# A hybrid decoder layer on one core: gated unit and gates projected for all tokens ahead of the mixers

## The chip, the cores and the metric

The kernel runs on one core of a Trainium2 chip. A core has TensorE (PE, matrix products into PSUM), VectorE (DVE), ScalarE (ACT), GpSimd (POOL) and SyncE (SP, which issues DMAs here), each with its own in-order list of instructions; they wait for each other on semaphores. The metric is the device time of one execution in microseconds, lower is better.

## What is computed

One layer on 1024 tokens of width 1024, in float32. The input is normalised (h), projected by one matrix, mixed by two branches, gated, projected and normalised again; then a feed-forward block with a 3-tap causal convolution.

```python
u = h @ w_in   # columns: conformer GLU (a, g) | z | x, B, C | dt | gate_a | gate_b
# conformer branch
v = a * sigmoid(g)
v = causal_dwconv(v, 31 taps)            # per channel, over positions
y_a = silu(layer_norm(v)) @ w_conv_out
# state-space branch: 4-tap causal conv and silu on x, B, C; dt = softplus(dt + bias)
# scan in chunks of 128 tokens, 4 groups of 8 heads, a state carried from chunk to chunk
y = scan(x, dt, B, C) + x * d_skip
y = y * silu(z); y = y * rsqrt(mean(y^2 per group))
y_b = (y * norm_w) @ w_ssm_out
# join
h = LN(alpha*h + (sigmoid(gate_a)*y_a + sigmoid(gate_b)*y_b) @ w_o)
h = LN(alpha*h + ConvFFN(h))
```

## The kernel before

**Precision.** Every float32 operand of a large product is split into a rounded part and a rest (ScalarE casts, VectorE subtracts), and a product is three matmuls (`mm3`, L180 to L182): part by part, part by rest, rest by part. A projection of one tile of 128 columns on 512 tokens (`project`) has 8 blocks along the width, so 24 matmuls. `weights` (L141) loads a tile of weights by SP into `wst` (three buffers) and splits it into `wsp` (three buffers).

**Two halves.** The tokens are worked off in two halves of 512, up to the first norm. `ln_first` (half 0) or `ln_in` (half 1) normalises four row tiles and transposes them into hT. `mixers` then projects dt, then for each of four groups g: B, C and four x tiles, each with the 4-tap convolution `conv4`; at g = 3 the first half of the state-space output, `ssm_out_first` (weights `w_so`, eight projections); two GLU tiles (`glu`, four projections, `w_ga` and `w_gg`); the scan `ssd_group`; in it at the end z (`z_gate`, four projections); and at low priority the 31 taps of the two GLU tiles (`conv31`, L545, 30 operations of 512 tokens each, the tail of half 0 kept in `v_halo`). After the loop come the eight tiles of gate a, their sigmoids sent to DRAM, with the last group's normalisation (`done(yT)`) behind the second of them.

`combine` projects the eight tiles of gate b and, interleaved, the second half of the state-space output (`w_sp`, which needs yT). It loads the tap results (tiles `cc`), normalises them over the channels (sums over tiles by POOL, L768 to L781; sums over partitions by TensorE), splits them into sT, and projects them (`w_co`); the joined result mixT goes to `out_proj`.

**The scan** of a group has four chunks in a row. A chunk transposes x (L593), loads a tile m of cumulated decays by POOL (L602, two buffers), turns it into decays on ScalarE (L607, L611) and VectorE (L623), updates the state (L632, L639) and multiplies (L642). At the end of a group come the skip, the gate, the squares, a sum by TensorE (L672), and a factor that goes out to DRAM and back (L680, L681).

**The feed-forward block** (`ffn_blocks`, `up_first`, `up_pair`, `down`) multiplies already by blocks: two column tiles of weights and all 1024 tokens make a 2 x 2 block product with seven products of half the width (12 matmuls each) in the place of eight. It needs sums of weight blocks (VectorE, L991 to L994) and of token blocks (made once, kept in `h1b` and `h1s`). For the first LEAD = 8 pairs the two products that need only the first half of the tokens are computed early (`up_first`), sent to DRAM and loaded again.

**Order.** The instructions of each engine are put in order ahead of time by a planner, by priority (the place in the program, moved by `tc.high_priority(offset=...)`) and by simulated readiness. Within `tc.manual_schedule` the named engines keep the program's order. Pools opened on the same side of the memory lie one on another, and a tile waits for the earlier tiles whose memory it takes. PSUM has two rings of four banks: `acc` for projections, `sm` for the scan and transposes.

Of the kernel before, what the change touches and what calls it, by code (L numbers as in the profile page):

```python
# [16 lines left out]
P = 128  # L17
D = 1024
# [6 lines left out]
LEAD = 8  # L25
HEADS = 32
# [28 lines left out]
def kernel(  # L55
# [39 lines left out]
    mean_stack = ExitStack()  # L95
    mean_w = mean_stack.enter_context(pool("mean", side="right")).tile([P, P], F32, name="mean_w")
    V.memset(mean_w, 1.0 / D)
    state_stack = ExitStack()
    statep = state_stack.enter_context(pool("states", side="right"))
    upper = statep.tile([P, P], F32, name="upper")  # L100
    make_upper_triangular(nc, upper, 1.0, diag=True)
    later = statep.tile([P, P], F32, name="later")
    make_lower_triangular(nc, later, 1.0, diag=False)
    ones = statep.tile([P, P], F32, name="ones")
    V.memset(ones, 1.0)
# [3 lines left out]
    a_log = statep.tile([P, HEADS], F32, name="a_log")  # L109
    nskip = statep.tile([P, 2, 16], F32, name="nskip")  # L110
    pick = statep.tile([P, 4, 4], F32, name="pick")
    V.memset(pick, 0.0)
    for c in range(4):
        V.memset(pick[:, c, c : c + 1], 1.0)
    u_halo = statep.tile([P, 24, 3], F32, name="u_halo")
    G.memset(u_halo, 0.0)
    v_halo = statep.tile([P, 8, KC - 1], F32, name="v_halo")
    G.memset(v_halo, 0.0)
    fold = statep.tile([2 * HEADS, HEADS], F32, name="fold")
    V.tensor_add(fold, ident[: 2 * HEADS, :HEADS], ident[: 2 * HEADS, HEADS : 2 * HEADS])  # L120
    states = [statep.tile([P, HALF], F32, name=f"state{g}") for g in range(GROUPS)]
    dts = [statep.tile([P, 4, HEADS], F32, name=n) for n in ("dtv", "wds")]
    edc = statep.tile([P, 2, 4, HEADS], F32, name="edc")
    cums = statep.tile([P, 4, HEADS], F32, name="cums")
# [10 lines left out]
    g_scr = [dram.tile([8, P, HALF], F32, name=f"g_scr{i}") for i in range(2)]  # L135
# [115 lines left out]
    def ln_first():  # L251

        hT = big_tile("hT0")
        et = mybir.EngineType
        with pool("lnin0", side="right") as pl:
            xts, raw = [], []
            with tc.high_priority(offset=8000), tc.manual_schedule(
                engines={et.Activation, et.DVE, et.PE}
            ):
                A.activation(out=pl.tile([P, 1], F32, name="warm"), in_=eps, func=AF.Sqrt)  # L260
                for t in range(4):
                    xt = pl.tile([P, D], F32, tag="x", bufs=4, name=f"x0_{t}")
                    SY.dma_start(xt, x[t * P : (t + 1) * P, :])
                    xts.append(xt)
                    if t == 1:
                        gb = [row(pl, RW_ING, D, "in_g"), row(pl, RW_INB, D, "in_b")]
                    for ct in ((), (), (CT_DT, CT_B), (CT_C,))[t]:
                        raw.append(raw_weights(ct, f"first{ct}"))
                SY.dma_start(pc[:, :PC_N], pcol[:, :PC_N])
                SY.dma_start(a_log, prow[RW_AL : RW_AL + HEADS].partition_broadcast(P))  # L270
                SY.dma_start(nskip.rearrange("p i k -> p (i k)"), pcol[:, PC_N:])
                mvs = [pl.tile([P, 1, 2], F32, name=f"mv_in{t}") for t in range(4)]
                rss = [pl.tile([P, 1], F32, name=f"rs_in{t}") for t in range(4)]
                work = pl.tile([P, D], F32, name="ln_work")
                pts = {}

                def stats(t):
                    st = pl.tile([P, 2, 6], F32, name=f"st_in{t}")
                    for q in range(2):
                        ln_part(pl, xts[t], st, q)  # L280
                    V.bn_aggr(out=mvs[t][:, 0, :], in_=st)
                    A.activation(out=rss[t], in_=mvs[t][:, :, 1], func=AF.Sqrt, bias=eps)

                def sums(t):
                    mean, var = mvs[t][:, 0, 0:1], mvs[t][:, 0, 1:2]
                    A.activation(out=work, in_=xts[t], func=AF.Identity, accum_out=var)
                    A.mul(mean, var, -1.0 / D)
                    A.activation(out=work, in_=xts[t], func=AF.Square, bias=mean, accum_out=var)
                    A.activation(out=rss[t], in_=var, func=AF.Sqrt, bias=eps, scale=1.0 / D)

                def norm(*ts):
                    for t in ts:
                        V.reciprocal(out=rss[t], in_=rss[t])
                        V.scalar_tensor_tensor(
                            out=xts[t], in0=xts[t], scalar=mvs[t][:, 0, 0:1], in1=gb[0],
                            op0=ALU.subtract if t < 2 else ALU.add, op1=ALU.mult,
                        )
                    for t in ts:
                        V.scalar_tensor_tensor(
                            out=xts[t], in0=xts[t], scalar=rss[t], in1=gb[1],  # L300
                            op0=ALU.mult, op1=ALU.add,
                        )
                        store(t)

                def store(t):
                    SY.dma_start(h_scr[0][t * P : (t + 1) * P, :], xts[t])

                def hi(t):
                    pts[t] = [transposed(xts[t], q) for q in (0, 4)]
                    for q, pt in zip((0, 4), pts[t]):  # L310
                        A.copy(hT[:, 0, q : q + 4, t * P : (t + 1) * P], pt)

                def lo(t):
                    for q, pt in zip((0, 4), pts[t]):
                        ks, ts = slice(q, q + 4), slice(t * P, (t + 1) * P)
                        V.tensor_tensor(
                            out=hT[:, 1, ks, ts], in0=pt, in1=hT[:, 0, ks, ts].bitcast(F32),
                            op=ALU.subtract,
                        )

                pss = [bank(1) for _ in range(3)]
                ws = []

                def columns(i, q, parts):
                    ts = slice(q * 256, (q + 1) * 256)
                    n = len(parts)
                    for m, (a, b) in enumerate(parts):
                        for k in range(KD):
                            if i:
                                w, ps = ws[i][:, a, k * P : (k + 1) * P], pss[i][:, ts]  # L330
                            else:
                                w, ps = ws[0][:, k, :], pss[0][: 2 * HEADS, ts]
                            TE.matmul(  # L333
                                ps,
                                w,
                                hT[:, b, k, ts],
                                start=(a, b) == (0, 0) and k == 0,
                                stop=(a, b) == (1 if i else 0, 0 if i else 1) and k == KD - 1,
                            )

                stats(0)
                stats(1)
                norm(0, 1)
                sums(2)
                hi(0)
                lo(0)
                ws.append(weights_side_by_side(raw[0], "c0_dt"))
                hi(1)
                lo(1)
                columns(0, 0, ((0, 0), (0, 1)))  # L350
                ws.append(split_weights(raw[1], "c0_b"))
                columns(1, 0, ((0, 0), (0, 1), (1, 0)))
                norm(2)
                sums(3)
                ws.append(split_weights(raw[2], "c0_c"))
                norm(3)
                hi(2)
                columns(2, 0, ((0, 0), (0, 1), (1, 0)))
                lo(2)
                hi(3)  # L360
                lo(3)
                for i in range(3):
                    columns(i, 1, ((0, 0), (0, 1)) + (((1, 0),) if i else ()))
        return hT, pss

    def ln_in():
        hT = big_tile("hT1")
        with pool("lnin1", side="right") as pl:
            xts = []
            with tc.high_priority(offset=6000):  # L370
                for t in range(4):
                    xt = pl.tile([P, D], F32, tag="x", bufs=4, name=f"x1_{t}")
                    SY.dma_start(xt, x[HALF + t * P : HALF + (t + 1) * P, :])
                    xts.append(xt)
# [138 lines left out]
    def glu(pl, hh, hT, i):  # L513
# [10 lines left out]
        if hh == 0:  # L524
            A.copy(v_halo[:, i, :], v[:, HALF:])
# [891 lines left out]
```

## Time and profile before

| | us |
|---|---|
| median of 3 runs | 1954.16 (1954.07 to 1954.42) |
| span of the profiled execution | 1951.6 |
| PE busy | 1926.3 (99%), 9128 matmuls |
| DVE busy | 1633.5 (84%) |
| ACT busy | 1105.9 (57%) |
| POOL busy | 133.7 (7%) |

The profile is of one execution. The runs' median is 2.6 us above its span, which goes from the first to the last instruction. Matmuls are pipelined: one of 512 columns is shown with about 0.39 us, but they follow each other more closely, so spacing, not duration, tells what one costs. The same holds, less so, for VectorE. A row of a timeline gives start, duration, engine, line, operation, result and operands; in brackets the idle time before it and what ended it. A row of grouped instructions gives count, total busy time and the mean duration of one in ns.

### The profile page before, as it was taken

What the parts mean: (1) busy time and instruction counts of PE and PEld (TensorE: products, weight loads), DVE (VectorE), ACT (ScalarE), POOL (GpSimd) and SP (SyncE); (2) the same over time, 40 slices, a digit from 0 to 9 for tenths busy, and PEclk for the clock granted to TensorE, in tenths of its full rate; (3) what the DMA queues carried; (4) which work ended last, traced back from release to release, by engine and by line L of the source; (5) the groups of instructions that cost most, each with busy time, mean ns of one, the idle gap of its engine ahead of it and who ended that gap; (6) DMA issues with size and microseconds to landing.
All of it is one profiled execution on the core that took longest, in us unless ns stands there. A gap on an engine that the chain in (4) does not pass through costs nothing.

```text
span 1951.6 us, 24929 instructions
## 1 busy us (share of the span) xinstructions
PE 1926.3 (99%) x9128; PEld 1575.7 (81%) x9128; DVE 1633.5 (84%) x2215; ACT 1105.9 (57%) x1841; POOL 133.7 (7%) x184
## 2 busy tenths in 40 slices
PE   7999999999999999999999999999999999999998
PEld 6888888887888887888888888888888888888886
DVE  7799999997666889999999956588998887878778
ACT  6767777664453367877765545365655454453442
POOL 0100000000400010000000040001000000011000
PEclk9999999999999999999999999999999999999999
DMA  6434343534546542424353454576443332368572
GB/s 223 132 114 130 108 136 118 177 100 141 178 128 215 207 131 96 143 104 136 107 174 108 139 180 129 159 267 243 156 157 108 113 103 90 113 230 268 180 253 108
DMA packets 104011, 297.68 MB, mean 153 GB/s; under 512 B 12432, under 2 KB 12464, under 8 KB 103888
## 3 DMA queue, kind: packets, MB, share of 16 engines
q1 hardware_dynamic: 87840, 244.68, 37.5%
q0 software_dynamic: 13744, 47.21, 7.8%
q10 hardware_dynamic: 2304, 4.20, 0.6%
q8 instruction: 71, 1.16, 0.3%
q14 instruction: 52, 0.43, 0.1%
HBM read 246.22 MB, written 49.82 MB: 152 GB/s over the span
## 4 chain that ended last, share of the span: by engine, by line
PE 78%; issue 11%; DVE 5%; DMA 3%; ACT 2%; POOL 1%; SPq 0%; DVEq 0%; ACTq 0%; POOLq 0%
PE acc L181 21%; PE acc L180 21%; PE acc L182 21%; PE sm L180 3%; PE sm L182 3%; PE sm L181 3%; PE sm L642 2%; PE sm L628 1%; PE sm L632 1%; DMA do<-wdown 1%; PE sm L593 1%; PE acc L333 1%; DMA m<-cum_scr 1%; DVE w_dn L1193 1%; DVE rows L244 1%
## 5 line engine op out<-in xcount | busy, mean ns | idle before, releaser
L545 DVE SCALAR_TENSOR_TENSOR c<-v,pc,c 128x512 f32<-128x512 f32 x480 | 346.1, 749 | 6.8 <-ACT c L534 5.6
L180 PE MATMUL acc<-hT,w_c 128*128 128x512 f32 x368 | 147.2, 400 | 0.0
L181 PE MATMUL acc<-hT,w_c 128*128 128x512 f32 x368 | 146.9, 399 | 0.0
L182 PE MATMUL acc<-hT,w_c 128*128 128x512 f32 x368 | 144.9, 394 | 0.0
L607 ACT ACTIVATE m<-m,cums 128x128 f32<-128x128 f32 x256 | 79.0, 398 | 64.5 <-DMA m<-cum_scr 60.7
L1052 DVE SCALAR_TENSOR_TENSOR fo<-u,pc,fo 128x1024 f32<-128x1024 f32 x88 | 111.3, 1289 | 0.0
L500 DVE SCALAR_TENSOR_TENSOR xbc<-u,pc,xbc 128x512 f32<-128x512 f32 x144 | 105.9, 751 | 1.1 <-ACT xbc L498 0.9
L180 PE MATMUL acc<-h1s,w_s 128*128 128x512 f32 x264 | 103.4, 392 | 0.2 <-ACT u L1036 0.2
L182 PE MATMUL acc<-h1s,w_s 128*128 128x512 f32 x264 | 103.0, 390 | 0.0
L182 PE MATMUL acc<-hT,w_z 128*128 128x512 f32 x256 | 102.8, 402 | 0.0
L181 PE MATMUL acc<-h1s,w_s 128*128 128x512 f32 x264 | 102.7, 389 | 0.0
L180 PE MATMUL acc<-hT,w_z 128*128 128x512 f32 x256 | 101.9, 398 | 0.4 <-ACT sig L521 0.4
L1192 ACT CAST w_dn<-dr 128x1024 fp32r<-128x1024 f32 (+1 forms) x73 | 60.7, 843 | 72.1 <-DVE dr L1122 42.5
L181 PE MATMUL acc<-hT,w_z 128*128 128x512 f32 x256 | 101.1, 395 | 0.0
L181 PEld LDWEIGHTS acc<-hT,w_c 128*128 128x128 f32 x368 | 69.2, 188 | 16.3 <-issue 3.1
L1193 DVE TENSOR_TENSOR w_dn<-dr,w_dn 128x1024 fp32r<-128x1024 f32 (+1 forms) x73 | 70.2, 971 | 13.8 <-ACT w_dn L1192 13.6
L182 PEld LDWEIGHTS acc<-hT,w_c 128*128 128x128 f32 x368 | 69.2, 188 | 15.6 <-issue 1.9
L180 PEld LDWEIGHTS acc<-hT,w_c 128*128 128x128 f32 x368 | 69.2, 188 | 15.5 <-issue 1.9
L147 DVE TENSOR_TENSOR w_c<-st_c,w_c 128x1024 fp32r<-128x1024 f32 x46 | 56.1, 1219 | 19.3 <-ACT w_c L146 19.3
L146 ACT CAST w_c<-st_c 128x1024 fp32r<-128x1024 f32 x46 | 48.3, 1051 | 40.7 <-PE acc L182 18.4
L180 PE MATMUL sm<-h1b,w_s 128*128 128x512 f32 x176 | 69.1, 393 | 0.0
L181 PE MATMUL sm<-h1b,w_s 128*128 128x512 f32 x176 | 69.0, 392 | 0.0
(382 smaller groups left out, 5596.2 us busy)
## 6 DMA issues: line engine op xcount, KB each, us to landing
st_c<-wcol SPq DMA_DIRECT2D x46, 512.0 KB, 3.5
st_z<-wz SPq DMA_DIRECT2D x32, 512.0 KB, 3.5
m<-cum_scr POOLq DMA_DIRECT2D x32, 512.0 KB, 4.7
st_wo<-wo SPq DMA_DIRECT2D x24, 512.0 KB, 4.1
ra<-wup SPq DMA_DIRECT2D x22, 512.0 KB, 3.8
rb<-wup SPq DMA_DIRECT2D x22, 512.0 KB, 3.3
t_scr<-fo POOLq DMA_DIRECT2D x22, 512.0 KB, 3.4
dr<-t_scr SPq DMA_DIRECT2D x44, 256.0 KB, 4.0
```

Source lines behind the costliest of these rows:

```text
L146: A.copy(w[:, 0, :], st)
L147: (eng or V).tensor_tensor(out=w[:, 1, :], in0=st, in1=w[:, 0, :].bitcast(F32), op=ALU.subtract)
L180: TE.matmul(ps, wa(0), xa(0), start=start, stop=False, skip_group_check=more)
L181: TE.matmul(ps, wa(0), xa(1), start=False, stop=False, skip_group_check=more)
L182: TE.matmul(ps, wa(1), xa(0), start=False, stop=stop, skip_group_check=more)
L500: V.scalar_tensor_tensor(out=o, in0=u[:, k : k + HALF], scalar=pc[:, wc + k : wc + k + 1], in1=o, op0=ALU.mult, op1=ALU.add,)
L545: V.scalar_tensor_tensor(out=accs[i], in0=v[:, k : k + HALF], scalar=pc[:, wc + k : wc + k + 1], in1=accs[i], op0=ALU.mult, op1=ALU.add,)
L607: A.activation(out=m[:, h, :], in_=m[:, h, :], func=AF.Relu, scale=-1.0, bias=cums[:, c, k : k + 1],)
L642: TE.matmul(py[h % 2 * HP : (h % 2 + 1) * HP, h // 2 * P : (h // 2 + 1) * P], xs[:, h * HP : (h + 1) * HP], m[:, h, :], start=True, stop=True,
L1052: V.scalar_tensor_tensor(out=o, in0=u[:, k : k + T], scalar=pc[:, wc + k : wc + k + 1], in1=o, op0=ALU.mult, op1=ALU.add,)
L1192: A.copy(w[:, 0, cs], src)
L1193: V.tensor_tensor(out=w[:, 1, cs], in0=src, in1=w[:, 0, cs].bitcast(F32), op=ALU.subtract)
```

## The change

**GLU and gates ahead of the mixers.** The 16 GLU tiles and the 16 gate tiles leave `mixers` and `combine`. They become 16 pairs of column tiles (eight pairs (a_i, g_i), four of gate a, four of gate b), each computed for all 1024 tokens by the seven block products that the feed-forward block has used, before the first mixer. The helpers are made general for it: `block_maker` (block sums of the tokens), `pair_first`, `pair_weights`, `pair`, `all_pairs`.

- `head` replaces `ln_first`: it normalises and transposes the first four row tiles, then, between the two early products of the first LEAD1 = 12 pairs, normalises the other four and makes the block sums. The columns dt, B, C of half 0 are no longer computed there; `first_columns` does so in both mixers.
- After each pair, `glu_and_gates` takes the sigmoid and, for GLU, the product with 1024 tokens, and sends the result to DRAM (`v_scr`, `g_scr`) by POOL.
- `ln_in` of half 1 loads the normalised rows from DRAM and only transposes and splits.

**Taps.** `conv31` now takes one channel tile, loads v from DRAM and stores by POOL. For four of the eight tiles (WHOLE = 4) it runs over all 1024 tokens (30 operations each), issued after the pairs 1, 5, 9 and 13 at lowered priority, with one buffer each for v and c. The other four run in halves in the mixers, one per group.

**Mixers and combine.** `done(yT)` of the last group stands directly behind the loop; the gates are loaded from DRAM. The constants and states of the scan are allocated after the pairs.

```diff
-                vs = [(i, glu(pl, hh, hT, i)) for i in (2 * g, 2 * g + 1)]
                 done = ssd_group(pl, hh, g, xT, BT, CT, lambda: z_gate(pl, hh, hT, g))
-                with tc.high_priority(offset=-1500):
-                    conv31(pl, hh, vs)
+                if WHOLE + g < 8:
+                    with tc.high_priority(offset=-1500):
+                        conv31(pl, WHOLE + g, hh * HALF, HALF)
+            done(yT)
+        return yT
...
             for j in range(8):
-                pg = bank(1)
-                project(pg, weights(wcol[CT_GA + j], f"gt{hh}_{j}"), hT)
-                ga = pl.tile([P, HALF], F32, tag="ya", bufs=2, name=f"gt{hh}_{j}")
-                A.activation(out=ga, in_=pg, func=AF.Sigmoid)
-                SY.dma_start(g_scr[hh][j], ga)
-                if j == 1:
-                    done(yT)
...
                 gb = pl.tile([P, HALF], F32, tag="gate", bufs=3, name=f"gb{hh}_{j}")
-                A.activation(out=gb, in_=pg, func=AF.Sigmoid)
+                SY.dma_start(gb, g_scr["gb"][j][:, hs])
...
+    def glu_and_gates(j, ug, uv):
+
+        if j < 8:
+            A.activation(out=uv, in_=uv, func=AF.Sigmoid)
+            V.tensor_mul(ug, ug, uv)
+            G.dma_start(v_scr[j], ug)
+            return
+        scr = g_scr["ga" if j < 12 else "gb"]
+        for i, u in enumerate((ug, uv)):
+            A.activation(out=u, in_=u, func=AF.Sigmoid)
+            G.dma_start(scr[2 * (j % 4) + i], u)
...
+        for t in range(4):
+            with tc.high_priority(offset=4000):
+                load(4 + t)
+            for j in range(3 * t, 3 * t + 3):
+                if j == 3 * t + (1 if t else 2):
+                    mv, rs = ln_stats(tp, [xts[4 + t]], f"in1_{t}")
+                    ln_apply(xts[4 + t], mv, rs, 0, *gb)
+                    store(4 + t)
+                    second_rows(t, xts[4 + t], V)
+                if j not in ws:
+                    lead_weights(j)
+                pair_first(fp, bl, first1_scr, j, [ws[j][:, i] for i in range(2)])
...
+    with pool("pairs1") as p1:
+        us = [p1.tile([P, T], F32, name=f"u1_{i}") for i in range(4)]
+        with pool("whole", side="right") as cp:
+
+            def taps(j):
+                if j % 4 == 1:
+                    with tc.high_priority(offset=-600):
+                        conv31(cp, j // 4, 0, T)
+
+            all_pairs(p1, us, 0, bl, first1_scr, srcs1, LEAD1, "p", None, glu_and_gates, taps)
+    st1.close()
...
-    yT = mixers(0, hT, pre)
+    yT = mixers(0, hT)
```

More of the change, by code (lines that the diff above doesn't have):

```diff
@@ L108 @@
     pc = const.tile([P, PC_N + 88], F32, name="pc")
[L109 to L124, printed above, removed]
     h_scr = [dram.tile([HALF, D], F32, name=f"h_scr{i}") for i in range(2)]
@@ L249, in ln_apply @@
         )
-    def ln_first():
-        hT = big_tile("hT0")
-        et = mybir.EngineType
[L255 to L364, printed above, removed]
@@ L1042, in up_pair, with all_pairs, made, taps_and_product @@
         V.tensor_tensor(out=uv[:, early], in0=pz, in1=s, op=ALU.subtract)
+        then(j, ug, uv)
+    def all_pairs(pl, us, off, bl, scr, srcs, lead, name, ws, then, after=None):
+        n = len(srcs)
+        def made(j, ws=None):
+            ws = ws or pair_weights(pl, srcs, j, lead, name)
+            return pair(pl, us, off, bl, scr, j, ws, then)
+        with tc.manual_schedule(engines={mybir.EngineType.PE}):
+            pairs = [made(0, ws)]
+            next(pairs[0])
+            next(pairs[0])
+            for j in range(1, n + 1):
+                if j < n:
+                    pairs.append(made(j))
+                    next(pairs[j])
+                next(pairs[j - 1], None)
+                if j < n:
+                    next(pairs[j])
+                if after:
+                    after(j - 1)
+    def glu_and_gates(j, ug, uv):
[8 more added lines that the diff above has]
+            G.dma_start(scr[2 * (j % 4) + i], u)
+    def taps_and_product(upp, kept, j, ug, uv):
         os = []
@@ L1276 @@
+    states = [statep.tile([P, HALF], F32, name=f"state{g}") for g in range(GROUPS)]
+    dts = [statep.tile([P, 4, HEADS], F32, name=n) for n in ("dtv", "wds")]
+    edc = statep.tile([P, 2, 4, HEADS], F32, name="edc")
+    cums = statep.tile([P, 4, HEADS], F32, name="cums")
+    SY.dma_start(a_log, prow[RW_AL : RW_AL + HEADS].partition_broadcast(P))
+    SY.dma_start(nskip.rearrange("p i k -> p (i k)"), pcol[:, PC_N:])
+    yT = mixers(0, hT)
     mixT = combine(0, hT, yT)
```

418 lines of the change are left out of this document (248 added, 170 removed).

## The prediction, made before the result was known

> **What bounds the kernel now.** I read the page's busy shares first, then the windows by stage, then TensorE's timeline around one mixer. From the page, total busy time and the two tap groups:
>
> ```profile
> span 1951.6 us, 24929 instructions
> PE 1926.3 (99%) x9128; PEld 1575.7 (81%) x9128; DVE 1633.5 (84%) x2215; ACT 1105.9 (57%) x1841; POOL 133.7 (7%) x184
> ...
> L545 DVE SCALAR_TENSOR_TENSOR c<-v,pc,c 128x512 f32<-128x512 f32 x480 | 346.1, 749 | 6.8 <-ACT c L534 5.6
> ...
> L1052 DVE SCALAR_TENSOR_TENSOR fo<-u,pc,fo 128x1024 f32<-128x1024 f32 x88 | 111.3, 1289 | 0.0
> ```
>
> TensorE is busy 99% of the span, so an instruction taken from it is worth its spacing only as long as the queue behind it stays full. The windows (length, then busy time of PE, PEld, DVE, ACT, POOL, clock, DMA) show the stages: mixers of the first half, mixers of the second, the first combine, the FFN pairs.
>
> ```profile
> 34.00:480.00 446.00, 446.00 (x2232) 361.27 (x2232) 409.67 (x587) 308.98 (x619) 20.05 (x35) 1.00 0.41 128
> 660.00:1122.00 462.00, 460.06 (x2311) 372.74 (x2309) 426.86 (x616) 307.54 (x567) 19.89 (x35) 1.00 0.41 130
> 480.00:570.00 90.00, 90.00 (x397) 73.12 (x396) 57.85 (x65) 46.70 (x62) 22.45 (x16) 1.00 0.46 152
> ...
> 1380.00:1500.00 120.00, 119.84 (x523) 97.90 (x522) 112.86 (x130) 65.71 (x80) 6.60 (x13) 1.00 0.44 149
> ```
>
> TensorE waits for nothing in any of them, though VectorE is at 92% in both mixers and at 94% in the FFN pairs. The reason is in TensorE's order. Below, the end of the first half's mixers: start, duration, line, operands.
>
> ```profile
> 369.71 0.39 PE L181 MATMUL acc<-yT,w_so 128*128 128x512 f32 x1
> ...
> 376.74 0.39 PE L182 MATMUL acc<-yT,w_so 128*128 128x512 f32 x1
> ...
> 399.71 0.39 PE L182 MATMUL acc<-hT,w_gg 128*128 128x512 f32 x1
> 399.94 0.60 PE L593 MATMUL sm<-ident,xbc 128*128 128x128 f32 x4
> ...
> 415.80 1.09 PE L642 MATMUL sm<-m,xs 128*64 128x128 f32 x16
> ...
> 461.80 1.09 PE L642 MATMUL sm<-m,xs 128*64 128x128 f32 x16
> 481.86 1.04 PE L672 MATMUL sm<-ss,pick 128*4 128x128 f32 x8
> ```
>
> The first two rows are 31 matmuls apart: 7.03 / 31 = 0.2268 us each, so one projection (24 matmuls) is 5.44 us. The order is the program's: the eight `w_so` projections, then the last GLU (`w_ga`, `w_gg`), and only then the scan of group 3, its four chunks from 399.94 to 462.89. The scan does not fill the machine: 70 projections in the 446 us window are 381 us, the other 65 us are mostly 16 chunks, 4.1 us each, while these four chunks lasted 62.9 us. What fills the rest is work that comes later in the program: z, gates a, gates b. That is the work the change takes away.
>
> **TensorE: what goes, and the head.** GLU and gates are 32 column tiles x 2 halves x 24 = 1536 matmuls. As 16 pairs of seven products of 12 they are 16 x 84 = 1344. 192 x 0.2268 = **-43.5 us**. Against it: the rows of the second half are now transposed in the head and again in `ln_in`, 32 transposes more, about 0.11 us apart (eight of L204 begin at 21.12 and the next work at 21.91, below): +3.6 us. The head itself:
>
> ```profile
> 15.77 2.63 PE L333 MATMUL acc<-hT,w_c_dt 128*64 128x256 f32 x16 [0.25 <-DVE w_c_dt L171]
> ...
> 21.12 1.03 PE L204 MATMUL sm<-ident,x 128*128 128x128 f32 x8
> 21.91 3.11 PE L333 MATMUL acc<-hT,w_c_c 128*128 128x256 f32 x24
> ...
> L180 PE MATMUL acc<-hT,w_c x368: 387/389/793, 35.0 to 975.3; 128*128 128x512 f32 x184
> 26.19 1.29 DVE L316 TENSOR_TENSOR hT<-sm,hT 128x512 fp32r<-128x512 f32 x2 [0.23 <-ACT hT L311]
> 17.12 1.23 DVE L160 TENSOR_TENSOR w_c_b<-st_first,w_c_b 128x1024 fp32r<-128x1024 f32 x1 [0.25 <-ACT w_c_b L159]
> ```
>
> Before, dt, B and C (64 matmuls of 512, 14.5 us) are worked off in the fill, so the 35.0 at which the next column starts is worth a start at 20.5. After, nothing can start before all four row tiles are in hT: 27.5 in the trace, less the B and C splits (1.23 each), plus one lead split, so about 26: +5.5 us. Without new waits: 1951.6 - 43.5 + 3.6 + 5.5 = **1917.2**.
>
> **VectorE in the pairs.** These rows price a pair (splits, adds, evacuations):
>
> ```profile
> L884 DVE TENSOR_TENSOR w_s<-ra,w_s 128x1024 fp32r<-128x1024 f32 x22 | 26.9, 1224 | 42.0 <-ACT w_s L883 42.0
> L1042 DVE TENSOR_TENSOR u<-sm,s 128x512 f32<-128x512 f32 x22 | 15.2, 692 | 6.4 <-PE sm L182 6.4
> ```
>
> A GLU pair has three 1024-wide operations (1.22) and seven 512-wide (0.69), 8.5 us; a gate pair has no product, 7.3; the four pairs without a lead add 1.9 each. Together 68 + 29 + 37 = 134 us. The four whole tap channels are 120 operations of 111.3 / 88 = 1.265, 152 us (in halves 240 x 0.721 = 173, so 21 us are saved). That makes 286 us beside (1344 - 288) x 0.2268 = 239 us of TensorE; the first taps also wait for pair 0 and a trip through DRAM. So 47 to 65 us of taps run on into the first mixers. There VectorE loses 24 splits, the GLU products and half the taps: 410 - 29 - 6 - 87 = 288, with the spill 335 to 353. TensorE's own work in a mixer is 48 projections, dt and the chunks: 261 + 4 + 65 = 330 us. I cost this spill at nothing, because the wait worked out next makes the stage longer than either; without that cover it costs up to 23 us. Lead products (288 matmuls, 65 us) cover the second half's layer norm and block sums (about 51 us of VectorE). Sigmoids, DRAM stores and the POOL and SP issues of the pairs sit beside TensorE's 239 us; ScalarE has about 8 us in each 15 us pair. The tap tiles' loads and stores now go by POOL (0.55 us an issue, row of L602 below); a store that waits there for its taps holds back an m load behind it, which I put into the second rival.
>
> **The wait that is added: the end of each mixer.** With GLU and gates gone, the order after `w_so` is: scan of group 3, z of group 3, then `w_sp`, which needs yT. How long are four chunks when TensorE has nothing else? The loop is POOL's load of the next m after the chunk's last matmul, ScalarE waiting for it, and the state products queued behind that on ScalarE:
>
> ```profile
> 1075.04 0.55 POOL L602 DMA_DIRECT2D m<-cum_scr  x1 [14.56 <-DVE c L545]
> 1079.39 2.45 ACT L607 ACTIVATE m<-m,cums 128x128 f32<-128x128 f32 x8 [3.41 <-DMA m<-cum_scr]
> 1081.75 1.71 ACT L622 ACTIVATE xsd<-sm,wds 128x64 f32<-128x64 f32 x8
> ```
>
> From 1075.04 to the end of the third row, 1083.46, are 8.4 us; exponent, product with the mask, L632, state and the next chunk's matmuls need some 4 more. I take 12.5 us a chunk; the ends are 10 (ScalarE's rows alone) and 15.7 (62.9 / 4). From the last chunk to yT:
>
> ```profile
> 484.56 0.52 POOL L680 DMA_DIRECT2D r_scr<-rr  x1 [52.38 <-DVE rr L678]
> 490.31 2.74 DVE L684 SCALAR_TENSOR_TENSOR xbc<-xbc,nskip,ss 128x512 f32<-128x512 f32 x4 [1.65 <-DMA ss<-r_scr]
> 492.97 1.89 DVE L197 TENSOR_TENSOR yT<-xbc,yT 128x512 fp32r<-128x512 f32 x3
> ```
>
> 462.9 to 493.7 is 30.8 us; some 6 us of it were taps and splits between, and L672 stood 4.7 behind gate matmuls: 20 us. TensorE has for these 50 + 20 us: the chunks 16, four z projections 21.8, and the first halves (group 2) of three `w_sp` tiles, as many as there are weight buffers, 8.2. It stands idle **24 us per half** (ends: 14 and 37); behind `w_sp` in its list stand `w_co` and the output projection, which need yT or sT themselves.
>
> **The conv branch behind it.** The c tiles take the memory of the xbc tiles, so their loads come when yT is done; then the norm, by POOL's sums:
>
> ```profile
> 497.34 4.29 SPq L761 DMA_DIRECT2D cc<-c_scr  x8
> 504.75 10.20 POOL L770 TENSOR_TENSOR mean<-mean,cc 128x512 f32<-128x512 f32 x6
> 518.19 10.73 POOL L781 TENSOR_TENSOR var<-var,csq 128x512 f32<-128x512 f32 x7 [3.25 <-ACT csq L780]
> 543.62 0.69 DVE L197 TENSOR_TENSOR sT<-cc,sT 128x512 fp32r<-128x512 f32 x1
> ```
>
> From 497.34 to the first part of sT, 544.31, are 47 us. Before, gates b and `w_sp` (87 us) hide them. After, `w_sp` alone has 35.3 us left and transposes of the next rows 3.6. I take **6 us per half** (8 by these rows, less sigmoids and table loads that go from ScalarE; ends 0 and 12).
>
> The sum: 1917.2 + 2 x (24 + 6) = 1977.2 in the profiled execution's time. Its runs' median, 1954.16, is 2.6 above its span, so **1980 us**.
>
> **A rule against the change.** What the clock does when TensorE stands still shows only at the end:
>
> ```profile
> 1941.59 0.39 PE L182 MATMUL acc<-last 128*128 128x512 f32 x1
> 1925.00:1950.00 25.00, 16.98 (x75) 13.72 (x74) 23.20 (x44) 1.63 (x6) 0.00 (x0) 0.91 0.43 168
> ```
>
> The last matmul ends at 1942.0; a mean clock of 0.91 over 25 us is 4.5 us at half, so the clock fell some 3.5 us after. The Trainium skill, "TensorE: Matmul & The Clock Gate", section Part 1: The HAM clock gate, states that after an idle window of about 3.4 us the array runs at half rate until a busy one has passed. The trace agrees on the fall; no row shows the return. By that page each of four waits would cost about 1.7 us more, an estimate that would make the sum 1987. The sum above goes without it.
>
> **Rivals.** (1) *Faster*: the scan of group 3 runs beside `w_so`. If TensorE's list puts its chunks between the 43.5 us of `w_so` (its inputs are ready by then), four chunks are covered and only the conv wait remains: 1917.2 + 12 + 2.6 = 1932; half-covered, 1945. It decides once the chunks begin 25 us or more before `w_so` ends. Against it: in both halves the trace has the chunks strictly behind `w_so` and GLU (399.71 and 399.94). For it: the list is laid out anew, and 10 us chunks alone bring 1960. (2) *VectorE becomes the bound*: the spilled taps come ahead of group 0's conv and scan, and the whole first mixer moves back by up to 23 us: 1995 to 2005. The FFN window (94% and no wait) speaks against; 335 to 353 us beside 330 speaks for. (3) The waits only eat the gain: 1950 to 1958.
>
> **How the numbers follow.** Forecast, waits of 20 to 45 us per half: 0.45, own range 1960 to 2010. Rival 2: 0.12. Rival 1: 0.36. Rival 3: 0.07. About 0.2% is what a measurement of this kernel can tell from no change. Faster 0.36, same 0.07, slower 0.57. The range takes in most of rival 1 and the upper ends without the highest chunk time in both halves: 1930 to 2012.
>
> **What would show it.** Matmul count down by 192 net of transposes; TensorE idle by 15 to 37 us between the end of group 3's z and the second halves of `w_sp`, in both halves; a shorter gap before `w_co`; first lead product near 26 us. If TensorE is above 98% busy through both mixers' ends, the forecast is wrong and rival 1 holds; if idle time lies in the pairs or ahead of group 0's chunks, rival 2.

## The result, and the profile after

The changed kernel takes **2121.15 us** (median of 3 runs, 2120.52 to 2123.51) against 1954.16: a ratio of 1.0859, 95% interval 1.084 to 1.0879. It is slower, as forecast, but by 167 us and not by 26; the time lies far above the range. The profiled execution spans 2121.8 us, 144.6 above the 1977.2 that the prediction's sum gave for it.

From the page of the changed kernel: the span, busy times, and the 40 slices of TensorE, VectorE and the granted clock.

```profile
span 2121.8 us, 24672 instructions
PE 1933.7 (91%) x8904; PEld 1564.7 (74%) x8904; DVE 1707.6 (80%) x2223; ACT 1115.4 (53%) x1874; POOL 164.9 (8%) x243
...
PE   5999999488897977999989896799999999999998
DVE  7579989887988768568899866867899878878868
...
PEclk9999999789998988999999998899999999999999
```

TensorE has fewer matmuls, yet its busy share fell from 99 to 91%, and the low digits lie between a sixth and two thirds of the span, in the mixers; the last third is as before. The windows of the changed kernel by stage (length, then busy PE, PEld, DVE, ACT, POOL, clock, DMA): lead products, pairs, the start of the first mixer up to its first z projection, the rest of that mixer, its end up to the first `w_co`, the second mixer, its end.

```profile
32.00:107.00 75.00, 70.65 (x300) 55.32 (x299) 50.10 (x73) 38.64 (x67) 0.13 (x1) 0.98 0.60 213
107.00:372.00 265.00, 264.59 (x1167) 217.94 (x1166) 234.78 (x258) 116.90 (x150) 18.79 (x38) 1.00 0.45 151
372.00:433.00 61.00, 22.70 (x85) 17.68 (x84) 49.82 (x51) 15.43 (x29) 3.35 (x8) 0.68 0.12 40
433.00:780.00 347.00, 313.94 (x1579) 247.29 (x1580) 280.76 (x405) 241.22 (x526) 23.84 (x45) 0.95 0.38 119
780.00:846.00 66.00, 42.26 (x178) 31.96 (x173) 50.63 (x57) 23.16 (x31) 25.00 (x16) 0.83 0.51 170
942.00:1311.00 369.00, 345.67 (x1772) 277.45 (x1772) 311.51 (x452) 250.32 (x497) 23.69 (x42) 0.97 0.39 125
1311.00:1378.00 67.00, 42.73 (x176) 32.43 (x171) 50.55 (x58) 23.75 (x32) 24.51 (x16) 0.79 0.52 169
```

Length less PE's busy time is TensorE's idle time: 0.4 us in the pairs, **38.3** at the start of the first mixer, **33.1** in the rest of it, 23.7 at its end, **23.3** in the second mixer, 24.3 at its end. The prediction had the two ends only.

Timelines of the changed kernel around its largest pause, by engine (start, duration, engine, line, operation, operands; in brackets the idle time before and what ended it):

```profile
379.40 39.59 DVE L563 SCALAR_TENSOR_TENSOR c<-v,pc,c 128x1024 f32<-128x1024 f32 x30 [4.41 <-ACT c L555]
418.91 0.17 DVE L437 TENSOR_SCALAR sp<-a_log 128x32 f32<-128x32 f32 x1
...
419.29 1.07 POOL L572 DMA_DIRECT2D c_scr<-c  x2 [45.23 <-DVE sp L437]
420.35 0.14 POOL L551 MEMSET v<- 128x30 f32 x1
420.40 0.55 POOL L552 DMA_DIRECT2D v<-v_scr  x1
...
423.95 0.81 ACT L555 ACTIVATE c<-v,pc 128x512 f32<-128x512 f32 x1 [40.45 <-DMA v<-v_scr]
...
431.84 0.79 PE L157 MATMUL acc<-h0b,w_z 128*128 128x512 f32 x1 [31.02 <-ACT w_z L123]
```

All 30 operations of the last whole channel run in one go on VectorE, with the first mixer's `conv4` and dt queued behind them. POOL's store of that channel waits for the last tap; POOL's load of the next v is queued behind the store; ScalarE waits 40.45 us for this v, with the cast of `w_z` behind it on its own queue; and TensorE waits for the cast. Three in-order queues pass one wait on; whether they or VectorE's own work decide is what experiment 2 asks. The 7.28 us of idle time before, from 372.7 on, come the same way: POOL loads the last whole channel's v (373.50) behind the store of the channel before it (372.38), which waits for that channel's last tap; ScalarE waits 4.34 us for this v (L555), and dt's copy (L419), for which TensorE waits, stands behind that.

The end of the first mixer, on TensorE: last chunk, sum of squares, second halves of `w_sp`, first `w_co`.

```profile
779.39 1.09 PE L660 MATMUL sm<-m,xs 128*64 128x128 f32 x16 [0.88 <-DVE m L641]
...
788.64 1.87 PE L690 MATMUL sm<-ss,pick 128*4 128x128 f32 x8 [8.16 <-DVE ss L685]
799.31 1.65 PE L157 MATMUL acc<-yT,w_sp 128*128 128x512 f32 x3 [8.80 <-ACT yT L173]
...
846.48 1.65 PE L157 MATMUL acc<-sT,w_co 128*128 128x512 f32 x3 [6.42 <-ACT sT L173]
```

This is the wait that was forecast: 8.16 + 8.80 between the last chunk and yT, 6.42 ahead of `w_co`.

### The profile page after: what moved, and what is told of

Same layout as the page of the kernel before. It is cut to its first block, busy times and chain, and to the rows that moved or that the text cites. A ratio compares the mean times of both kernels' runs of the same rounds, so it can differ in the third digit from the quotient of the medians.

```text
span 2121.8 us, 24672 instructions
## 1 busy us (share of the span) xinstructions
PE 1933.7 (91%) x8904; PEld 1564.7 (74%) x8904; DVE 1707.6 (80%) x2223; ACT 1115.4 (53%) x1874; POOL 164.9 (8%) x243
## 4 chain that ended last, share of the span: by engine, by line
PE 47%; DVE 6%; DMA 4%; ACT 3%; issue 2%; POOL 1%; SPq 0%; DVEq 0%; POOLq 0%; ACTq 0%
PE acc L158 12%; PE acc L159 12%; PE acc L157 12%; PE sm L157 3%; PE sm L158 3%; PE sm L159 3%; DMA m<-cum_scr 1%; DMA st_wo<-wo 1%; ACT m L625 1%; PE sm L660 1%; DMA first_scr<-first 0%; POOL mean L771 0%; PE sm L646 0%; DVE rows L221 0%; DVE cc L789 0%
## 5 line engine op out<-in xcount | busy, mean ns | idle before, releaser
L563 DVE SCALAR_TENSOR_TENSOR c<-v,pc,c 128x512 f32<-128x512 f32 (+1 forms) x360 | 332.7, 924 | 24.6 <-ACT c L555 21.2
L157 PE MATMUL acc<-h1s,w_rs 128*128 128x512 f32 x264 | 103.1, 391 | 0.0
L159 PE MATMUL acc<-h1s,w_rs 128*128 128x512 f32 x264 | 103.1, 390 | 0.0
L158 PE MATMUL acc<-h1s,w_rs 128*128 128x512 f32 x264 | 102.7, 389 | 0.0
L625 ACT ACTIVATE m<-m,cums 128x128 f32<-128x128 f32 x256 | 78.9, 400 | 44.7 <-DMA m<-cum_scr 44.7
L157 PE MATMUL acc<-hT,w_c 128*128 128x512 f32 x192 | 78.7, 410 | 14.6 <-ACT xbc L530 7.7
L157 PE MATMUL acc<-h0b,w_c 128*128 128x512 f32 x192 | 81.0, 422 | 11.1 <-ACT zs L583 6.8
L157 PE MATMUL acc<-h0b,w_z 128*128 128x512 f32 x128 | 52.2, 408 | 31.1 <-ACT w_z L123 31.0
L158 PE MATMUL acc<-h0b,w_c 128*128 128x512 f32 x192 | 79.0, 411 | 0.0
L159 PE MATMUL acc<-h0b,w_c 128*128 128x512 f32 x192 | 78.6, 409 | 0.0
L158 PE MATMUL acc<-hT,w_c 128*128 128x512 f32 x192 | 77.6, 404 | 0.0
L159 PE MATMUL acc<-hT,w_c 128*128 128x512 f32 x192 | 77.4, 404 | 0.0
L157 PE MATMUL acc<-h0s,w_ps 128*128 128x512 f32 x192 | 74.8, 390 | 0.4 <-ACT u L983 0.4
L158 PE MATMUL acc<-h0s,w_ps 128*128 128x512 f32 x192 | 74.7, 389 | 0.0
L159 PE MATMUL acc<-h0s,w_ps 128*128 128x512 f32 x192 | 74.7, 389 | 0.0
L157 PE MATMUL sm<-h1b,w_rs 128*128 128x512 f32 x176 | 69.1, 393 | 0.0
```

Source lines behind the costliest of these rows:

```text
L157: TE.matmul(ps, wa(0), xa(0), start=start, stop=False, skip_group_check=more)
L158: TE.matmul(ps, wa(0), xa(1), start=False, stop=False, skip_group_check=more)
L159: TE.matmul(ps, wa(1), xa(0), start=False, stop=stop, skip_group_check=more)
L563: V.scalar_tensor_tensor(out=c, in0=v[:, k : k + n], scalar=pc[:, wc + k : wc + k + 1], in1=c, op0=ALU.mult, op1=ALU.add,)
L625: A.activation(out=m[:, h, :], in_=m[:, h, :], func=AF.Relu, scale=-1.0, bias=cums[:, c, k : k + 1],)
```

## The experiments

Times are of single runs where no ratio stands beside them. The kernel before took 1951.7 to 1952.8 us beside these kernels (1954.16 beside the changed one), so differences of 2 us say nothing. The edits are against the changed kernel unless another is named.

**1. The whole channels' taps**

```diff
-        for k in range(KC - 1):
+        for k in range(1 if n == T else KC - 1):
```

> Leaves out 29 of the 30 tap operations of each of the four whole tap tiles (116 operations of about 1.27 us), all else as in the changed kernel. Theory A (the stand-still between the pairs and the first mixer, 7.3 + 31.0 us of idle TensorE near 373 to 432, comes from whole taps that spill over the end of the pairs): that idle time falls below 5 us and the time falls from 2121 to 2055 to 2080. Rival B (it comes from the constants and tiles of the mixer that wait for memory of the pairs): idle there stays above 25 us, time above 2095.

2053.48 us, 67.7 less. The pause at the start of the first mixer is gone (38.3 to 0.0 us of idle TensorE), and from the last pair product to the last chunk of half 0 it is 356 us and not 424: the whole channels' taps cost **68 us** there, and nothing hid them. 56.5 us of this are idle time of TensorE (38.3 + 33.1 against 14.9). The windows of this kernel's two mixers:

```profile
390.00:712.00 322.00, 307.12 (x1586) 243.71 (x1585) 269.96 (x386) 234.70 (x515) 23.88 (x45) 0.98 0.39 126
...
876.00:1241.00 365.00, 344.32 (x1771) 277.11 (x1769) 310.62 (x449) 246.73 (x495) 23.72 (x42) 0.98 0.39 126
```

14.9 and 20.7 us of idle time are left in them.

**2. POOL's queue at that pause**

```diff
-            G.dma_start(v, v_scr[i][:, n0 - KC + 1 : n0 + n])
+            SY.dma_start(v, v_scr[i][:, n0 - KC + 1 : n0 + n])
...
-            G.dma_start(v[:, KC - 1 :], v_scr[i][:, :n])
+            (G if n == T else SY).dma_start(v[:, KC - 1 :], v_scr[i][:, :n])
```

> The half tap tiles load v by SP and not by POOL, so that the first of them no longer stands behind the last whole tile's store in POOL's list. Theory A1 (ScalarE is held 40 us by that load and with it the casts of the z weights): the 31 us of idle shrink below 10 us, time 2075 to 2095. Rival A2 (VectorE itself is held by 30 whole taps in a row, so that the dt steps and the 4-tap convolutions are late whatever ScalarE does): some 20 us or more of idle stay at this place, time 2105 to 2121.

2108.8 us. ScalarE no longer waits for the v of the half tile, but it waits as long for VectorE, whose dt step (L438) stands behind the taps, and TensorE's wait for `w_z` only falls from 31.0 to 26.3 us (total, times, longest):

```profile
ACT sp L439 <- DVE sp L438: 35.8, 1, 35.8
...
PE acc L157 <- ACT w_z L123: 26.3, 1, 26.3
```

So it is VectorE's run of taps that holds the mixer; the queue adds 4.7 us to this wait and 12 us to the time.

**3. A third buffer for m**

```diff
-            m = pl.tile([P, 8, P], F32, tag="m", bufs=2, name=f"m{nm}")
+            m = pl.tile([P, 8, P], F32, tag="m", bufs=3, name=f"m{nm}")
```

> Three buffers for the tile m of decays in the place of two, so its load is issued a chunk earlier. Theory C (in the mixers TensorE stands still because ScalarE waits in order for m, and the PSUM evacuations and casts behind it are late): ScalarE's wait for m falls from 44.7 us below 20, idle TensorE in the two mixers (31 and 21 us) falls by a third or more, time 2085 to 2108. Rival D (VectorE's load or the chain from chunk to chunk sets the pace): time within 8 us of 2121.

2102.11 us, 19 less and in theory C's range, but ScalarE's wait for m fell from 44.7 to 42.9 us only. TensorE's idle time from the last pair product to the last chunk fell from 71.4 to 65.2 us, that in the second mixer from 23.3 to 15.0. The buffer helps; that it does so through this wait is not borne out.

**4. All taps in halves, in the mixers**

```diff
-WHOLE = 4
+WHOLE = 0
...
+                    for i in (2 * g, 2 * g + 1):
+                        conv31(pl, i, hh * HALF, HALF)
```

(and two buffers each for v and c; the taps beside the pairs go)

> All eight tap tiles in halves in the mixers, two per group with two buffers, as before the change; no whole tiles. Theory A: the idle time ahead of the first mixer goes (below 8 us), and VectorE's work in a mixer rises by 87 us to 375, beside 330 of TensorE, so that the mixers get longer; together 2060 to 2095. Rival B: idle ahead of the mixer stays, time above 2121.

2148.17 us, a miss: nothing stands ahead of the first mixer, but the idle time inside the mixers grows to 55.4 and 50.5 us. The taps were moved, not hidden.

**5. Gate a back at the mixers' ends** (with experiment 1's edit, and 12 pairs)

```diff
-            done(yT)
+            for j in range(8):
+                pg = bank(1)
+                project(pg, weights(wcol[CT_GA + j], f"gt{hh}_{j}"), hT)
...
+                if j == 1:
+                    done(yT)
```

> As e1_one_tap (29 of 30 operations of each whole tap tile left out), and gate a projected at the end of each mixer again, eight projections, so 12 pairs in the place of 16. Beside e1_one_tap at 2053. Theory E (after the last chunk TensorE stands still because nothing is left that can run until yT and then sT are there; 25 us of idle per half, some 32 us with the slow clock): idle between the last chunk and w_co falls below 3 us per half; TensorE gets 10.9 us more; time 1995 to 2015. Rival F (the wait is bound by something that the gates would not cover, so that they only come on top): idle stays above 15 us per half, time above 2040.

2020.39 us, 5 above the expected range, 33 below experiment 1 although 48 matmuls more are run. The windows from the last chunk to `w_co`:

```profile
653.00:728.00 75.00, 64.39 (x287) 50.26 (x283) 55.88 (x62) 30.43 (x41) 24.86 (x16) 0.97 0.59 194
1204.00:1277.00 73.00, 66.79 (x293) 53.42 (x291) 54.21 (x62) 32.00 (x41) 24.89 (x16) 1.00 0.60 205
```

Of the 25 us of idle time in each, 10.6 and 6.2 are left; the two waits for yT are gone, the one for sT stays, which was the miss.

**6. No taps at all**

```diff
-        for k in range(KC - 1):
+        for k in range(1):
```

> Leaves out 29 of 30 operations of all tap tiles, the halves in the mixers too, so VectorE loses another 87 us per mixer. Beside e1_one_tap at 2053 (idle inside the two mixers 15 and 21 us). Theory D (inside the mixers VectorE's load makes weights, convolutions and state late): that idle falls below 5 us per mixer, time 2005 to 2025. Rival C (the chain of the scan, with ScalarE waiting in order for m, makes it): idle stays above 12 us per mixer, time above 2035.

2003.90 us, 49.6 below experiment 1. The windows of its first mixer, that mixer's end, and the second mixer:

```profile
389.00:692.00 303.00, 300.23 (x1585) 240.39 (x1583) 198.79 (x270) 241.27 (x522) 19.96 (x35) 1.00 0.40 129
692.00:758.00 66.00, 41.74 (x168) 31.85 (x168) 50.74 (x58) 23.66 (x32) 24.53 (x16) 0.83 0.51 171
854.00:1192.00 338.00, 336.64 (x1762) 271.44 (x1762) 235.67 (x333) 252.40 (x500) 23.75 (x42) 1.00 0.42 136
```

The idle time inside the mixers falls to 2.8 and 1.4 us, the one at the end stays at 24.3: the halves of the taps cause the first and have no part in the second. ScalarE's wait for m falls with them, here in experiment 1 and then in this one (total, times, longest):

```profile
ACT m L625 <- DMA m<-cum_scr: 43.1, 20, 7.1
```

```profile
ACT m L625 <- DMA m<-cum_scr: 21.9, 14, 3.4
```

So about half of that wait goes with the taps; a third buffer (experiment 3) had left it as it was.

**7. Only the GLU in pairs**, gates as in the kernel before; taps in halves, two beside the pairs and six in the first mixer, two beside the output projection and six in the second

```diff
-    srcs1 += [(wcol[c + 2 * k], wcol[c + 2 * k + 1]) for c in (CT_GA, CT_GB) for k in range(4)]
...
+                for i in ((2, 3), (4,), (5, 6), (7,))[g]:
...
+                        conv31(pl, i, hh * HALF, HALF)
```

(and 8 lead pairs, two buffers each for v and c)

> The whole computation, with GLU alone in pairs (8), gates a and b projected in mixers and combine as before the change; taps in halves, two tiles of half 0 beside the pairs, their half 1 beside the output projection of half 0, six per mixer. TensorE saves 8 x 12 matmuls, 21.8 us; the head costs 18 us as measured in the changed kernel, tails and the stretch ahead of the first mixer nothing. Theory E with A: 1945 to 1965, idle after the last chunk below 3 us. Rival F: above 1990.

2097.78 us, ratio 1.0745 (1.0728 to 1.0763), a miss by over 130 us. At the ends nothing is idle any more, but inside the mixers:

```profile
234.00:610.00 376.00, 328.08 (x1615) 258.54 (x1615) 310.45 (x450) 240.15 (x521) 25.63 (x49) 0.93 0.35 115
610.00:728.00 118.00, 118.00 (x526) 96.41 (x523) 69.75 (x81) 58.12 (x76) 22.46 (x16) 1.00 0.43 148
819.00:1248.00 429.00, 375.96 (x1841) 300.37 (x1839) 373.75 (x550) 255.88 (x506) 27.61 (x49) 0.92 0.36 118
```

47.9 and 53.0 us, with VectorE at 83 and 87%, less than the 92% beside which the kernel before waited for nothing.

**8. Taps three beside the pairs and five in the mixers**, GLU and gate b in pairs, three buffers for m

```diff
-                for i in ((2, 3), (4,), (5, 6), (7,))[g]:
+                for i in ((3, 4), (5,), (6,), (7,))[g]:
```

(the diff is against experiment 7, cut to the taps in the mixers)

> The whole computation: 12 pairs (GLU and gate b), gate a at the end of each mixer, three tap tiles of half 0 beside the pairs and five in the mixer, the three of half 1 beside the output projection of half 0, three buffers for m. TensorE saves 32.7 us, the head costs 18, the insides of the mixers some 10 to 20 each. Theories A and E: 1955 to 1985, idle ahead of the first mixer below 5 us, after the last chunk below 3 us. Rival (VectorE still decides): above 2000.

2132.52 us, ratio 1.0921 (1.0903 to 1.0939), the second miss. 47 us are idle in the first mixer and 81 in the second; the largest single wait, 23.4 us for dt, stands where three tiles' taps of half 1 run ahead of that mixer. It is passed on by ScalarE: its first operation of a tap tile (L555) waits 20.82 us for the store of the tile whose buffer it takes, and dt's copy (L419) stands behind it.

**9. Experiment 7 with the tap tiles off POOL's queue**

```diff
-            G.dma_start(v[:, KC - 1 :], v_scr[i][:, :n])
+            SY.dma_start(v[:, KC - 1 :], v_scr[i][:, :n])
...
-            G.dma_start(c_scr[(n0 + q) // HALF][i], c[:, q : q + HALF])
+            SY.dma_start(c_scr[(n0 + q) // HALF][i], c[:, q : q + HALF])
```

> As e7_glu_pairs (whole computation, only the eight gated unit pairs ahead of the mixers), but every tap tile's v is loaded and its result stored by SP's queue, as the result was before the change, so that GpSimd's queue holds only the mixers' own transfers. Question: what holds TensorE for 101 us inside the mixers of e7 (47.9 in the first, 19.9 and 33.2 in the second). Theory Q, the m loads stand behind tap tiles' loads and stores in GpSimd's queue: the idle time inside the mixers falls below 40 us and the time below 2040. Rival V, VectorE itself, taps queued ahead of the scan and the weight splits: at least 80 us of it are left and the time is 2075 to 2105.

2083.16 us, as rival V has it; the two mixers:

```profile
234.00:604.00 370.00, 334.08 (x1668) 265.65 (x1668) 310.39 (x450) 247.06 (x528) 20.37 (x39) 0.95 0.37 120
802.00:1234.00 432.00, 372.55 (x1841) 297.96 (x1839) 378.42 (x556) 255.74 (x506) 19.91 (x35) 0.92 0.36 117
```

95.4 of the 101.0 us stay (35.9 + 59.5). The queue is not the main cause, though the time is 15 us less without the tap tiles in it. That VectorE is the cause, this run alone does not show; the next one tests it.

**10. Experiment 7 without taps**

```diff
-        for k in range(KC - 1):
+        for k in range(1):
```

> As e7_glu_pairs, but 29 of the 30 tap operations of every 31-tap tile are left out (those beside the pairs and those in the mixers), so that VectorE has some 300 us less work. Theory V and the tail theory together: TensorE's idle time inside the mixers falls from 101 us to below 12, after the last chunks it stays near nothing as in e7, and the time is the kernel before's less 96 matmuls (22 us) plus the head (about 18) and a little for slow matmuls after pauses: 1950 to 1970. Rival: the order of the mixers (scratch loads of m, ScalarE in its order) holds TensorE without taps too: over 30 us idle inside the mixers and a time over 1985.

1962.89 us, as expected; its two mixers:

```profile
233.00:546.00 313.00, 309.31 (x1609) 247.28 (x1610) 200.97 (x271) 246.82 (x526) 20.45 (x36) 0.99 0.41 130
...
755.00:1100.00 345.00, 342.43 (x1791) 275.76 (x1791) 239.62 (x340) 261.11 (x509) 25.31 (x45) 1.00 0.42 139
```

6.3 us are idle in them. The tap tiles' loads, their first operation on ScalarE and their stores are still there, so it is VectorE's tap operations (294 us of its busy time) that held the mixers. The time is what hiding all of them could at best bring in this form, and still 11 us above the kernel before in the same job (1951.74).

**11. Experiment 5 without taps**

```diff
-        for k in range(1 if n == T else KC - 1):
+        for k in range(1):
```

(against experiment 5)

> As e5_gate_a_last (12 pairs ahead, gate a at each mixer's end), with 29 of the 30 tap operations left out of every 31-tap tile, not of the whole ones alone. If the costs found so far add, this is e6_no_taps (2003.9) less what gate a at the mixers' ends brought (33 us from e1 to e5): 1960 to 1980, with under 8 us of TensorE's idle time inside the mixers and under 18 us after the last chunks of both halves together. Rival: the 144 matmuls saved show once VectorE and the tails no longer hold TensorE: below 1950, faster than the kernel before.

1966.18 us: the costs add (2003.9 less 33 would be 1971), and the 144 matmuls saved do not show as a gain even here (before: 1952.77).

**12. Fewer taps in the mixers**: experiment 9 with three tiles beside the pairs, five in the first mixer, four beside half 0's `w_co`, four in the second mixer

```diff
                 V.tensor_add(mb[j], mb[j], ga)
+                if not hh and j < 4:
+                    conv31(pl, j, HALF, HALF)
```

> As e9_queue (whole computation), but with fewer tap tiles in the mixers: in half 0 three of eight stand beside the pairs and five in the mixer (before: two and six), in half 1 four stand beside out-projection's lead-in, the conv output products of half 0, where VectorE is about half idle, and four in the mixer (before: two queued at its start, six in it). Theory V, VectorE's amount of work inside the mixers: of the 95 us that TensorE idles there in e9 30 to 50 us go (three tiles of 20 us less, not all of it uncovered), and the time is 2020 to 2055. Rival: the order of the mixers, not the amount: at least 85 us stay and the time is over 2070.

2097.65 us, a miss for both: inside the mixers 28 us of the 95 are gone, just below what the amount theory has, and all of it in the second (59.5 to 28.7); the first, with a tile fewer, has 38.8 after 35.9. The time is 14 us longer than experiment 9's. One wait in the output projection took most of it back. Timelines by engine:

```profile
798.58 17.43 DVE L563 SCALAR_TENSOR_TENSOR c<-v,pc,c 128x512 f32<-128x512 f32 x26
...
814.58 1.78 SPq L572 DMA_DIRECT2D c_scr<-c  x2
816.47 2.98 SPq L409 DMA_DIRECT2D x<-h_scr  x4
...
820.10 1.94 PE L181 MATMUL sm<-ident,x 128*128 128x128 f32 x8 [23.79 <-DMA x<-h_scr]
```

SP's queue holds the stores of the last tap results ahead of the loads of half 1's rows, and VectorE does these taps last of all, 26 in a row up to 816.01; TensorE stands for 23.79 us, waiting for rows that the head had stored long before. The tap tiles also lie in `combine`'s pool, whose memory later tiles take; whether the queue or the memory held the loads was not separated.

## Why the prediction was wrong

**Step that failed: the spill of VectorE's work, "I cost this spill at nothing, because the wait worked out next makes the stage longer than either; without that cover it costs up to 23 us."** Its size was right (47 to 65 us of taps; in the trace 38 of the 120 operations, 48 us, stand behind the last pair product), its price was not: 68 us (experiment 1), idle time and a slower clock included. The step compared sums of a stage, VectorE's 335 to 353 us beside TensorE's 330, and let the wait at the end absorb the rest. But the taps stand in one run of 39.59 us ahead of everything that the first mixer needs from VectorE, and the wait at the end comes 350 us later, so neither hides the other. The second rival named this mechanism at this place, "the whole first mixer moves back", and priced it by the same sums; its sign, idle time ahead of group 0's chunks, is what the windows show. So the forecast direction came out, but most of the 167 us is not what it rested on: the waits at the ends are 48 us of idle time.

**A term that was missing: the halves of the taps inside the mixers**, 49.6 us (experiment 1 against 6). The prediction explained that "TensorE waits for nothing in any of them, though VectorE is at 92%" by the filler, "work that comes later in the program", but it priced the loss of this filler at the mixers' ends alone; inside them it added up VectorE's work (288 us, half the taps among it) beside TensorE's 330 and put its lateness at nothing. VectorE's share is lower now, 81 and 84% in the long windows of the two mixers, and TensorE waits 33 and 23 us. Without taps it does not. That gate and GLU projections covered the same lateness before fits this and the filler that the prediction itself described; it is argued, not shown, since no run put them back between the chunks (experiments 5 and 7 put gates back behind the scan, where they cover the end alone).

**The wait at the mixers' ends: right in its mechanism, a little large.** 24 + 6 us per half were forecast; the windows give 23.7 and 24.3 in all, 17 + 6 us by the rows. Four chunks of group 3 took 45 us, 11.3 each, against 12.5. Experiment 5 shows the cause: projections that need no yT, put there, remove the wait for it. The first rival, chunks beside `w_so`, did not come about.

**The head: too small.** The first lead product was to start near 26 us.

```profile
25.75 1.23 DVE L201 BATCH_NORM_STATS2 st_in<-x 128x6 f32<-128x512 f32 x2
26.90 2.34 DVE L124 TENSOR_TENSOR w_ue<-st_ue,w_ue 128x1024 fp32r<-128x1024 f32 x2
29.16 1.28 DVE L338 SCALAR_TENSOR_TENSOR x<-x,rs_in,in_b 128x1024 f32<-128x1024 f32 x1
...
30.58 1.94 PE L181 MATMUL sm<-ident,x 128*128 128x128 f32 x8 [7.76 <-DVE x L338]
32.34 1.65 PE L157 MATMUL acc<-h0b,w_ue 128*128 128x512 f32 x3
```

Statistics of the second half's first rows and two lead splits came ahead of the last row's norm (L338): 6.3 us late. The lead products with their transposes last 75 us against 65.3 + 3.6, which is 6.1 more.

**The matmul count: right in kind.** 9128 to 8904 in the records, 224 less: 192 by the pairs, 64 because the first half's dt, B and C of group 0 take 512 columns at once in the place of two times 256, and 32 transposes more. The pairs run without a pause (264.59 of 265). It was worth its 43.5 us only where the queue stays full, and the prediction said so.

**The clock: left out of the sum, and larger than its estimate.** TensorE after the 7.28 us of idle time that stand ahead of the dt products at 379.94:

```profile
382.37 0.63 PE L158 MATMUL acc<-h0b,w_c 128*128 128x512 f32 x1
382.80 0.63 PE L159 MATMUL acc<-h0b,w_c 128*128 128x512 f32 x1
...
387.26 0.39 PE L158 MATMUL acc<-h0b,w_c 128*128 128x512 f32 x1
387.49 0.40 PE L159 MATMUL acc<-h0b,w_c 128*128 128x512 f32 x1
```

The spacing is 0.43 us for 12 matmuls, then 0.23. The Trainium skill, "TensorE: Matmul & The Clock Gate", Part 1: The HAM clock gate, states half rate after an idle window of some 3.4 us until a busy window has passed, the windows being free-running. The rows agree now that the rate falls and that it returns (mean granted clock 1.00 from 373 to 376.5, 0.50 from 377 to 386.9, 1.00 from 387 on). But the slow stretch from the first dt product at 379.94 to 387.0 is 7.1 us, about two such windows and not one, so the 1.7 us that the prediction estimated for a wait were here rather 2.4 (12 x 0.20). In all, 186 matmuls of 512 columns in the changed kernel start 0.36 to 0.60 us before the next one, against 36 before: an estimate of 30 us (150 x 0.20), spread over all the waits.

**The sum again.** 1977.2 + 68 (whole channels) + 50 (halves) + 12 (head) - 12 (ends: 48 idle against 60) + 4 (idle time left in the mixers without taps) + 11 (slow matmuls left without taps: 91 in experiment 6 against 36, 0.20 each) = 2110. Some 12 us of the 2121.8 are not in this sum; 3.4 of them are a second wait for sT, inside the `w_co` products (1.7 per half), the others stay unassigned. A part of what experiments 1 and 6 saved is itself slow matmuls, so those are not counted twice here.

**What stays open.** How the taps could be laid so that no mixer waits: four layouts (experiments 4, 7, 8, 12) put them elsewhere and each found a new place to wait. That the taps make the waits inside the mixers is shown (experiments 6 and 10), and that the queue of their transfers counts too; that fewer of them make less of it is shown for the second mixer of experiment 12 and not for its first. Whether an order of VectorE exists that hides them was not settled. By which engine VectorE's lateness reaches TensorE inside the mixers was followed only at single waits. No kernel tried beats the kernel before, and experiments 10 and 11 show that in these two forms, 8 and 12 pairs, a perfect hiding of the taps would not have been enough.

## What to carry to other kernels

Work that seems redundant on the bounding engine may be the filler that lets other engines be late: before it is taken away, ask in each place what stands next in the queue and which engine that waits for. Compare two engines by the order of their queues at the place, not by their sums over a stage: 48 us of spilled work cost 68 us, though the sums differed by at most 23. A store that waits for low-priority work holds every load behind it on its queue, so such stores belong on a queue with nothing urgent behind them.

## What was not expected of the hardware

After an idle time of 4.4 us (ahead of 1091.65 in the second mixer) as after one of 31.0 us, TensorE ran at half rate for 5.3 and 6.4 us, 12 matmuls each (0.43 us apart, then 0.23). So a wait of 4.4 us cost nearly as much in clock as one seven times as long, and many waits of this length are dearer than their sum. Shorter ones went both ways: after one of 2.21 us (ahead of 543.94) the next eight matmuls were slow too, after one of 3.02 us (ahead of 497.93) none was.
